# Low ranks, bonus and group mean of RWKV scans as two passes of rounded parts in place of one float32 product

## The chip, the core and the metric

One core of one Trainium2 chip runs the whole program. The time is device microseconds (us) of that core; a kernel's time is the median of its runs. TensorE (PE) multiplies, ScalarE (ACT) and VectorE (DVE) work on tiles in on-chip memory, GpSimd (POOL) does slower elementwise work, and SyncE (SP) issues all loads and stores, in order.

## The reference

A two-layer encoder runs on two sequences (512 and 256 positions, width 1024). Layer 1 has a bidirectional RWKV-7 time mix with 16 heads of 64. What matters here, cut:

```python
g = sigmoid(xg @ g1) @ g2                                   # rank 128
for d in range(2):                                          # forward, backward
    w_log = -softplus(-(w0[d] + tanh(xw @ w1[d]) @ w2[d])) - 0.5      # rank 64
    a = heads(sigmoid(a0[d] + (xa @ a1[d]) @ a2[d]))                  # rank 64
    k_d = k * (1.0 + (a - 1.0) * k_a)
    outs.append(wkv7_scan(r, decay, k_d, v, -kk, kk * a, reverse=(d == 1)))
    bonus.append(sum(r * k_d * r_k, axis=-1, keepdims=True) * v)
y = outs[0] + outs[1]
mean = mean(y, axis=-1); y = (y - mean) * rsqrt(var(y) + eps)         # per head of 64
y = (y * lnx_w + lnx_b + bonus[0] + bonus[1]) * g @ w_o
```

"Second stage" is the product with `w2[d]` or `a2[d]`; the first stage, `xw @ w1`, is made earlier and kept as the low rank tiles.

## The kernel before

Activations lie with features on the 128 partitions and positions along the row. Dense products don't use float32 operands: `split` makes of a tile a rounded part `hi` (type float32r, an ACT copy) and the rest `lo` (a DVE subtraction), and `mms` (L340 to L342) adds three products: hi·hi, hi·lo, lo·hi. The scans' own products are float32, each of which is two matmul instructions in the trace.

`mixer1_scan` works through 12 units: 8 units of two heads for the long sequence (512 positions) and 4 units of four heads for the short one (two tiles of 256 positions). A unit goes through four generators: `prep` (loads k, r, v and the second-stage weights, decay, keys, bonus), `inverse` (the inverse of the chunks' triangular matrices, with many 32x32 products), `scan` (8 chunk steps) and `tail` (group norm, bonus, gate). `weave` interleaves scan of unit u, inverse of u+1, tail of u-1 and prep of u+2 in proportion to given weights. `fill` is dense work with no tie to the scans (feed-forward, projections, memory keys, output projection); `pour` puts pieces of it between the scan's steps. Then a scheduler with its own timing model sets each engine's final order. Every engine works its list in order, so an instruction that waits holds up all behind it.

The places that change, with their names in the trace:

- `second(i, d)` in `prep`, four times a unit: `wide` (L1121) multiplies 64 rows of `w2r` with 64 rows of the rank tile (`l0w`, `l0a`, `l1w`, `l1a`; both directions in one tile, 64 rows each) into a PSUM tile `e`; ACT takes tanh of it (L1158).
- The bonus, once a unit: a DVE product makes `rk` (0/1 block matrix times `r_k`), `wide` multiplies it with `ks` (tile name `th`), and DVE multiplies by v (L1210).
- The mean in `tail`, once a unit: `wide` with the 0/1 matrix `blk` sums y over each head, and DVE subtracts 1/64 of it (L1426).
- The gate's product `g2` with `l0g` or `l1g` also goes through `wide`.
- The low ranks of the long sequence go to memory in `rwkv_in` and are read back at the scans' start; those of the short one are made by `small_low` within `fill`.

Of the kernel before, what the change touches and what calls it, by code (L numbers as in the profile page):

```python
# [37 lines left out]
class Net:  # L38
# [781 lines left out]
    def mixer1_tables(self, c):  # L820
        nc = self.nc
        self.tri = c.tile([128, 2, 128], F32, name="tri2")
        with self.tc.tile_pool(name="tri", bufs=1) as t:
# [3 lines left out]
            for d in range(2):  # L827
                for r in range(2):
                    for q in range(2):
# [12 lines left out]
                             self.par[:, n:n + KT].unsqueeze(1).to_broadcast([128, 12, KT]))  # L842
        self.blk = c.tile([128, 128], F32, name="blk")
        nc.vector.memset(self.blk, 0.0)
        for h in range(2):
            nc.vector.memset(self.blk[64 * h:64 * h + 64, 64 * h:64 * h + 64], 1.0)
        self.id32 = c.tile([128, 32], F32, name="id32")
# [19 lines left out]
    def rwkv_in(self, x, save, L):  # L867
# [97 lines left out]
    def small_low(self, x, L, mix, rstd, nxt):  # L965
# [12 lines left out]
        for j, i in enumerate(LOW):  # L978
            if j == len(LOW) - 1:

                t = self.big("x")
                nc.gpsimd.tensor_copy(t, x[KT - 1])
                x[KT - 1] = t
            ps = [self.pmm.tile([128, self.W], F32, name="mm") for _ in range(2)]
            for r in range(0, KT, 4):
                wr = [[next(ws) for _ in range(4)] for _ in ps]
                for k in range(0, 4, n):
                    for t, w4 in zip(ps, wr):
                        for q in range(k, k + n):
# [4 lines left out]
            t, b = L["wag".index(LOW[i])], self.big("pt")  # L994
# [9 lines left out]
            self.low_end(i, t, t)  # L1004
        yield

# [61 lines left out]
    def head_rsqrt(self, sq, eps, scale, clamp, big, pool):  # L1068
# [3 lines left out]
        for t in range(4):  # L1072
            nc.tensor.matmul(ps[:, t, :], lhsT=sq[:, t * 128:(t + 1) * 128], rhs=self.blk[:, 0:128:64],
                             start=True, stop=True)
# [13 lines left out]

    def mixer1_scan(self, L, rkv, zs, bvs, fill):

# [26 lines left out]
        def wide(lhsT, rhs, pool):  # L1117

            ps = pool.tile([128, W], F32, name="e")
            for (c, l), r in zip(lhsT, rhs):  # L1120
                nc.tensor.matmul(ps[:, c], lhsT=l, rhs=r, start=True, stop=True)  # L1121
            return ps

        def prep(u, o):

            q, parts = units[u]
            np_, p0 = len(parts), parts[0][0]
            Lq = L[q]
            io = {}
# [19 lines left out]
            ks = None  # L1149

            def second(i, d):
                rows = lohi[d]
# [50 lines left out]
            nc.gpsimd.tensor_mul(ks, ks, r)  # L1203
            rks = []
            for p, c in parts:
                rk = ph.tile([128, 128], F32, name="rk", bufs=2)
                nc.vector.tensor_scalar_mul(rk, self.blk, self.p("rw_rk", 0, p))
                rks.append((c, rk))
# [103 lines left out]
        def scan(u, o):  # L1312
# [25 lines left out]
            def ahead(i):  # L1338
# [6 lines left out]
                for d in range(2):  # L1345

                    nc.scalar.activation(uv[:, :, d, :], ps, AF.Copy, scale=self.blk[:, 64 - 64 * d:65 - 64 * d])
                bt = ph.tile([128, 2, 2, 128], F32, name="BT", bufs=2)
# [68 lines left out]
        def tail(u, o):  # L1417

            q, parts = units[u]
            y = o["y"]  # L1420
            bv = tt("bv2")
            nc.sync.dma_start(bv, bvs[u])
            g2 = self.tl.tile([128, 256], F32, name="g2", bufs=1)[:, :128 * len(parts)]
            nc.sync.dma_start(g2, a["rw_g2"][0][:, 128 * parts[0][0]:128 * (parts[-1][0] + 1)])
# [10 lines left out]
            ps = wide([(c, g2[:, 128 * j:128 * j + 128]) for j, (p, c) in enumerate(parts)],  # L1435
                      [L[q][2]] * len(parts), self.pp)
            nc.vector.tensor_mul(y, y, ps)
# [49 lines left out]
    def mixer1(self, l=1):  # L1487
        tc, nc = self.tc, self.nc
        with tc.tile_pool(name="spill", bufs=1, space=bass.MemoryType.DRAM) as dram:
# [4 lines left out]
            bvs = [dt(f"bvs{u}", 512) for u in range(12)]  # L1494
            Ld = [dt(f"l0{n}", SP) for n in "wag"]
            with self.phase():
                self.save_x(xsave, 0)
                g = self.at(SP).rwkv_in([x[:, :SP] for x in self.x], rkv[0], Ld)

# [12 lines left out]
            with tc.tile_pool(name="lora", bufs=1, side="right") as lora, \  # L1512
# [4 lines left out]
                with tc.tile_pool(name="tail", bufs=1, side="right", reuse_waits="tile") as self.tl, self.phase(), ExitStack() as c:  # L1517
                    L = [[lora.tile([128, s1 - s0], F32, name=f"l{q}{n}") for n in "wag"] for q, (s0, s1) in enumerate(SEQS)]
                    for d, t in zip(Ld, L[0]):
                        nc.sync.dma_start(t, d)  # L1520
# [4 lines left out]
                    y = self.mixer1_scan(L, rkv, zs, bvs, self.fill(l, f, xsave, rkv, L, zs))  # L1525

# [158 lines left out]
```

## Time and profile before

| | before |
|---|---|
| median of 3 runs (lowest, highest) | 3052.07 us (3044.27, 3055.18) |
| profiled execution: its own time, span in the trace | 3050.94 us, 3049.0 us |
| busy over the span: PE, DVE, ACT, POOL | 2920.7, 1691.6, 1283.1, 669.1 us |
| the scans, 1250 to 2260 us of the span: PE, DVE, ACT busy | 953.53, 544.36, 568.78 us |
| granted TensorE clock in the scans, as a share of full speed | 0.95 |

Busy time of PE counts the modelled drain of a matmul, which overlaps the next; what a product costs PE is the distance from its start to the next one's start. [...]

### The profile page before, as it was taken

To read this page: it belongs to the slowest core of one execution; us is meant where nothing else is said; L and a number is where in the kernel's file an instruction comes from. 1 tells how busy PE (TensorE), PEld (TensorE's weight loads), DVE (VectorE), ACT (ScalarE), POOL (GpSimd) and SP (SyncE) were. 2 spreads that over 40 slices of the span, in tenths; PEclk is the share of its full clock that TensorE was granted. 3 is DMA by queue.
4 is the path that set the end of the run, shared out by engine and by line. 5 is a ranking of instruction groups with operands and counts; after the bars stand their busy time and mean duration, and the time that the engine had idled before them with its cause. 6 is when DMAs were issued, how large, how long until landed. Compare 5 with 4: busy or idle time off the path is not lost.

```text
span 3049.0 us, 55768 instructions
## 1 busy us (share of the span) xinstructions
PE 2920.7 (96%) x22624; PEld 2467.5 (81%) x22624; DVE 1691.6 (55%) x3008; ACT 1283.1 (42%) x2507; POOL 669.1 (22%) x672
## 2 busy tenths in 40 slices
PE   7999999999999989899989999999989999999997
PEld 6888888888888878777877777777778888888886
DVE  8888647464454596455576545544435564334244
ACT  3333435342232376455656665555444342122122
POOL 4124004020000110232473334444353020000001
PEclk9999999999999999999998999999999999999999
DMA  4224332121265667765435553222352112212111
GB/s 127 58 83 136 114 120 92 51 68 56 97 198 189 209 202 241 256 191 148 147 110 156 152 155 94 76 79 71 112 175 74 59 42 70 69 56 70 63 62 56
DMA packets 362144, 349.23 MB, mean 115 GB/s; under 512 B 42528, under 2 KB 291488, under 8 KB 361888
## 3 DMA queue, kind: packets, MB, share of 16 engines
q1 hardware_dynamic: 361888, 345.68, 36.6%
q8 instruction: 177, 2.90, 0.4%
q14 instruction: 79, 0.65, 0.1%
HBM read 269.06 MB, written 71.83 MB: 112 GB/s over the span
## 4 chain that ended last, share of the span: by engine, by line
PE 79%; DVE 10%; DMA 4%; ACT 3%; issue 3%; POOL 1%; SPq 0%; POOLq 0%; DVEq 0%; ACTq 0%
PE mm L340 21%; PE mm L341 20%; PE mm L342 20%; PE C L1336 3%; PE g L1227 2%; PE y L1336 2%; PE e L1121 2%; PE mm L331 1%; PE sm L331 1%; DVE xs L228 1%; DVE lt L1252 1%; DVE wlo L270 1%; DVE xr L1253 1%; PE py L331 1%; DMA tlo<-low 1%
## 5 line engine op out<-in xcount | busy, mean ns | idle before, releaser
L340 PE MATMUL mm<-xs,whi 128*128 128x512 f32 x2128 | 748.6, 353 | 12.1 <-ACT whi L269 11.0
L341 PE MATMUL mm<-xs,whi 128*128 128x512 f32 x2128 | 751.4, 354 | 4.2 <-DVE xs L228 3.0
L342 PE MATMUL mm<-xs,wlo 128*128 128x512 f32 x2128 | 746.8, 351 | 4.2 <-DVE wlo L270 4.1
L269 ACT CAST whi<-wraw 128x512 fp32r<-128x512 f32 (+1 forms) x492 | 301.9, 616 | 838.8 <-PE mm L341 782.3
L270 DVE TENSOR_TENSOR wlo<-wraw,whi 128x512 fp32r<-128x512 f32 (+1 forms) x492 | 364.4, 743 | 399.9 <-ACT whi L269 371.0
L340 PEld LDWEIGHTS mm<-xs,whi 128*128 128x128 f32 x2128 | 403.0, 190 | 69.6 <-ACT whi L269 11.4
L342 PEld LDWEIGHTS mm<-xs,wlo 128*128 128x128 f32 x2128 | 401.4, 189 | 61.8 <-DVE wlo L270 5.9
L341 PEld LDWEIGHTS mm<-xs,whi 128*128 128x128 f32 x2128 | 402.8, 189 | 58.8 <-DVE xs L228 3.9
L192 POOL TENSOR_TENSOR acc<-acc,sq 128x768 f32<-128x768 f32 (+2 forms) x72 | 114.1, 1585 | 1269.4 <-issue 896.0
L341 PE MATMUL mm<-fb,thi 128*128 128x256 f32 (+1 forms) x720 | 232.7, 323 | 1.1 <-DVE fb L225 1.1
L340 PE MATMUL mm<-hid,whi 128*128 128x512 f32 (+1 forms) x528 | 186.1, 356 | 2.3 <-ACT hid L224 2.3
L341 PE MATMUL mm<-hid,whi 128*128 128x512 f32 (+1 forms) x528 | 187.6, 356 | 0.0
L342 PE MATMUL mm<-hid,wlo 128*128 128x512 f32 (+1 forms) x528 | 186.3, 354 | 0.0
L340 PE MATMUL mm<-fb,thi 128*128 128x256 f32 x528 | 167.9, 318 | 9.3 <-ACT thi L301 9.0
L301 ACT CAST thi<-traw 128x512 fp32r<-128x512 f32 (+1 forms) x202 | 122.6, 609 | 115.8 <-PE mm L341 62.2
L342 PE MATMUL mm<-fb,tlo 128*128 128x256 f32 x528 | 156.4, 299 | 6.3 <-DMA tlo<-low 4.5
L341 PEld LDWEIGHTS mm<-fb,thi 128*128 128x128 f32 x720 | 143.5, 199 | 5.4 <-DVE fb L225 1.3
L340 PE MATMUL mm<-fa,thi 128*128 128x512 f32 (+1 forms) x304 | 125.4, 414 | 0.3 <-ACT fa L224 0.2
L340 PEld LDWEIGHTS mm<-fb,thi 128*128 128x128 f32 x528 | 106.0, 201 | 22.4 <-ACT thi L301 13.2
L342 PEld LDWEIGHTS mm<-fb,tlo 128*128 128x128 f32 x528 | 105.7, 201 | 11.1 <-DMA tlo<-low 5.9
L340 PEld LDWEIGHTS mm<-hid,whi 128*128 128x128 f32 x528 | 99.5, 189 | 17.6 <-ACT hid L224 2.7
L342 PE MATMUL mm<-fa,tlo 128*128 128x512 f32 (+1 forms) x304 | 110.5, 364 | 1.7 <-DMA tlo<-low 1.7
(374 smaller groups left out, 5701.9 us busy)
## 6 DMA issues: line engine op xcount, KB each, us to landing
wraw<-in_ffn_wgu_dram SPq DMA_DIRECT2D x44, 1024.0 KB, 5.2
tlo<-low SPq DMA_DIRECT2D x128, 256.0 KB, 3.2
low<-wlo SPq DMA_DIRECT2D x120, 256.0 KB, 2.8
wraw<-in_ffn_wdown_dram SPq DMA_DIRECT2D x23, 1024.0 KB, 5.2
traw<-in_ffn_wgu_dram SPq DMA_DIRECT2D x56, 256.0 KB, 3.7
wraw<-in_ab_w_in_dram SPq DMA_DIRECT2D x24, 512.0 KB, 3.9
wraw<-in_ca_wkv_dram SPq DMA_DIRECT2D x8, 1024.0 KB, 5.6
kvd<-kv SPq DMA_DIRECT2D x32, 256.0 KB, 2.0
```

The source lines that it names most:

```text
L192: nc.gpsimd.tensor_add(acc, acc, sq)
L228: nc.vector.scalar_tensor_tensor(lo, src, g, hi.bitcast(F32), op0=OP.mult, op1=OP.subtract)
L269: nc.scalar.copy(hi[:, :, :m], raw[:, k0:k1, j:j + m])
L270: nc.vector.tensor_sub(lo[:, :, :m], raw[:, k0:k1, j:j + m], hi[:, :, :m].bitcast(F32))
L301: nc.scalar.copy(hi[:, :n], raw[:, :n])
L331: self.nc.tensor.matmul(ps, lhsT=a[u], rhs=b[v], start=k == 0 and j == 0, stop=k == len(pairs) - 1 and j == 2)
L340: nc.tensor.matmul(ps[:, s0:s1], lhsT=wh, rhs=xh[:, s0:s1], start=start and k == 0, stop=False)
L341: nc.tensor.matmul(ps[:, s0:s1], lhsT=wh, rhs=xl[:, s0:s1], start=False, stop=False)
L342: nc.tensor.matmul(ps[:, s0:s1], lhsT=wl, rhs=xh[:, s0:s1], start=False, stop=stop and k == n - 1)
L1121: nc.tensor.matmul(ps[:, c], lhsT=l, rhs=r, start=True, stop=True)
L1227: nc.tensor.matmul(ps[h][:, j, d, :], lhsT=flat(BK[d][lohi[h], c]), rhs=flat(AR[d][lohi[h], c]), start=True, stop=True)
L1336: last[0] = nc.tensor.matmul(o, lhsT=lhsT, rhs=rhs, start=start, stop=False, skip_group_check=True)
```

## The change

Three groups of float32 products become sums of float32r products with 128 rows.

- Second stages. The low rank of each direction is kept as `hi` and `lo` parts, stacked on 64 + 64 rows of one tile (`lw`, `la`). The weights are loaded twice, into both halves of `w2r`, and split into `w2h` and `w2l`. The product is `w2h` with the stacked tile, plus `w2l` with the stacked tile. `fetch` loads and splits one weight at a time, the next one right behind the product that used the last.
- Bonus. `ks` times `r_k` is split into `kh` and `kl` by ACT and DVE; both are multiplied with the 0/1 matrix `blkr`.
- Mean. y is split into `yh` and `yl`; both are multiplied with `cen`, which is the identity minus 1/64 of the block matrix, so that the product is y minus its mean, which DVE copies out. `tail` has one step more.

Gate, variance and all other products stay. The diff, cut:

```diff
+        self.blk = c.tile([128, 2], F32, name="blk")
+        self.blkr, self.cen = [c.tile([128, 128], F32R, name=n) for n in ("blkr", "cen")]
...
-            nc.sync.dma_start(L["wag".index(LOW[i])], t)
+            if LOW[i] == "g":
+                nc.sync.dma_start(L["g"], t)
+            else:
+                for to, part in zip(L[LOW[i]], self.split(t, tag="xl", bufs=8)):
+                    nc.sync.dma_start(to, part.bitcast(F32))
...
-                nc.tensor.matmul(ps[:, c], lhsT=l, rhs=r, start=True, stop=True)
+                n = len(l)
+                for i in range(n):
+                    nc.tensor.matmul(ps[:, c], lhsT=l[i], rhs=r[i], start=i == 0, stop=i == n - 1)
...
+        def low(q):
+            if q not in ranks:
+                s0, s1 = SEQS[q]
+                ranks[q] = {n: [ph.tile([128, SP], F32R, name=f"l{n}{d}", bufs=1)[:, :s1 - s0] for d in range(2)] for n in "wa"}
+                for n, ts in ranks[q].items():
+                    for d, t in enumerate(ts):
+                        for i, p in enumerate(Ld[q][n]):
+                            nc.sync.dma_start(t[64 * i:64 * i + 64].bitcast(F32), p[64 * d:64 * d + 64])
...
-            w2 = ph.tile([128, 2, 256], F32, name="w2r", bufs=1)
-            for i, n in enumerate(("rw_w2", "rw_a2")):
-                for d in range(2):
-                    nc.sync.dma_start(w2[64 * d:64 * d + 64, i, :128 * np_], a[n][0, d][:, 128 * p0:128 * (p0 + np_)])
...
+            def fetch():
+                if order:
+                    i, d = order.pop(0)
+                    w2 = [ph.tile([128, 256], F32R, name="w2" + s, bufs=1)[:, :128 * np_] for s in "hl"]
+                    raw = ph.tile([128, 256], F32, name="w2r", bufs=1)[:, :128 * np_]
+                    for rows in lohi:
+                        nc.sync.dma_start(raw[rows], a[("rw_w2", "rw_a2")[i]][0, d][:, 128 * p0:128 * (p0 + np_)])
+                    nc.scalar.copy(w2[0], raw)
+                    nc.vector.tensor_sub(w2[1], raw, w2[0].bitcast(F32))
+                    w2s.append(w2)
...
-                ps = wide([(c, w2[rows, i, 128 * j:128 * j + 128]) for j, (p, c) in enumerate(parts)],
-                          [Lq[i][rows]] * np_, self.pp)
+                l, w2 = Lq["wa"[i]][d], w2s.pop(0)
+                ps = wide([(c, [t[:, 128 * j:128 * j + 128] for t in w2]) for j, (p, c) in enumerate(parts)],
+                          [(l, l)] * np_, self.pp)
+                fetch()
...
-                nc.vector.tensor_scalar_mul(rk, self.blk, self.p("rw_rk", 0, p))
+                nc.scalar.activation(hi[:, c], ks[:, c], AF.Copy, scale=self.p("rw_rk", 0, p))
+                nc.vector.scalar_tensor_tensor(lo[:, c], ks[:, c], self.p("rw_rk", 0, p), hi[:, c].bitcast(F32),
+                                               op0=OP.mult, op1=OP.subtract)
-            nc.vector.tensor_mul(bv, wide(rks, [ks[:, c] for _, c in parts], self.pp), v)
+            nc.vector.tensor_mul(bv, wide([(slice(0, W), [self.blkr] * 2)], [(hi, lo)], self.pp), v)
...
-            ps = wide([(slice(0, W), self.blk)], [y], self.pp)
-            nc.vector.scalar_tensor_tensor(y, ps, -1.0 / 64, y, op0=OP.mult, op1=OP.add)
+            nc.scalar.copy(hi, y)
+            nc.vector.tensor_sub(lo, y, hi.bitcast(F32))
+            yield
+            ps = wide([(slice(0, W), [self.cen] * 2)], [(hi, lo)], self.pp)
+            nc.vector.tensor_copy(y, ps)
...
-            weave((part(scan, u), 17), (part(inverse, u + 1), 16), (part(tail, u - 1), 4), (part(prep, u + 2), 12))
+            weave((part(scan, u), 17), (part(inverse, u + 1), 16), (part(tail, u - 1), 5), (part(prep, u + 2), 12))
```

The scheduler's order moves with it. On SP at the scans' start (`iok`, `ior`, `iov` are unit 0's k, r, v; `tlo` and `traw` are weights of the fill), before:

```order
L941 DMA r_9432<-pt 128x512
L1133 DMA iok<-k_9433 128x512
L1133 DMA ior<-r_9425 128x512
L1133 DMA iov<-v_9441 128x512
L1138 DMA w2r<-in_rw_w_dram 64x128 x2
L1138 DMA w2r<-in_rw_a_dram 64x128 x2
L303 DMA tlo<-low_7665 128x512
L294 DMA traw<-in_ffn_wgu_dram 128x4x128
```

and now, where `l0wh` and the like are the parts of the long sequence's ranks in memory:

```order
L952 DMA r_9432<-pt 128x512
L1153 DMA lw_11415<-l0wh 64x512
L1153 DMA lw_11415<-l0wl 64x512
L1153 DMA lw_11416<-l0wh 64x512
L1153 DMA la_11417<-l0ah 64x512
...
L1165 DMA iok<-k_9433 128x512
L1165 DMA ior<-r_9425 128x512
L1165 DMA iov<-v_9441 128x512
L1188 DMA w2r<-in_rw_w_dram 64x128 x2
L303 DMA tlo<-low_7665 128x512
```

Eight loads of ranks stand ahead of `iok`, and the two loads of the `a` weights have moved behind the fill's `tlo`.

On ACT, in the first direction of unit 3's prep (`th<-e,half` is the tanh of a second stage, `R` and `uv` belong to the scan's chain of unit 1), before:

```order
L1379 COPY uv<-C 64x128
L1428 ACTIVATE ysq<-y 128x512
L1235 COPY XL_11384<-G 32x128 x4
L1158 ACTIVATE th<-e,half 128x512
L301 CAST thi<-traw 128x512
L1163 ACTIVATE th<-th 128x512
L431 ACTIVATE th<-g 128x256
L1169 ACTIVATE E<-cu 128x8x64
L1171 ACTIVATE cu<-cu 128x512
```

and now:

```order
L1171 ACTIVATE kksq<-kk 128x512
L1316 COPY Y<-g_13473 128x512
L1420 COPY R<-C 128x128
L301 CAST thi<-traw 128x512
L1189 CAST w2h<-w2r 128x128
L1202 ACTIVATE th<-e,half 128x512
L1207 ACTIVATE th<-th 128x512
L1213 ACTIVATE E<-cu 128x8x64
L1423 COPY uv<-C 64x128
```

A cast of the next weight, which waits for its load and for PE's last use of `w2h`, now stands ahead of the tanh, and a `uv` copy of the scan stands behind both.

On PE at the mean of unit 0, before:

```order
L1352 MATMUL e<-ident,bk_12589 128x128
L1121 MATMUL e<-y,blk 128x512
L1336 MATMUL C<-R,Xinv_11383 128x64 x2
L340 MATMUL mm<-fb,thi 128x256
L341 MATMUL mm<-fb,thi 128x256
```

and now:

```order
L342 MATMUL mm<-fb,tlo 128x256
L1140 MATMUL e<-yh,cen 128x512
L1140 MATMUL e<-yl,cen 128x512
L1388 MATMUL e<-ident,v_13963 128x128 x2
L1380 MATMUL y<-G,uv 64x64 x2
L1380 MATMUL C<-uv,BT 64x64 x4
```

The one product stood between a transpose and a product of the scan's own chain; the two passes stand together, behind products of the fill and ahead of the scan's next transposes.

## Rows read from the trace of the kernel before

**Rows 1.** Busy time by engine in the scans: PE, PEld (weight loads), DVE, ACT, POOL, clock, DMA.

```profile
1250.00:2260.00 1010.00, 953.53 (x11785) 768.73 (x11783) 544.36 (x1187) 568.78 (x1286) 408.28 (x470) 0.95 0.44 131
```

**Rows 2.** The chain that ended last, in the scans, by line.

```profile
by line: PE mm L340 9.9%; PE C L1336 9.2%; PE mm L342 7.8%; PE mm L341 7.7%; PE g L1227 6.9%; PE y L1336 6.2%; PE e L1121 6.0%; issue 3.4%; DVE lt L1252 2.9%; DVE xr L1253 2.7%; DMA tlo<-low 1.9%; DMA traw<-in_ffn_wgu_dram 1.7%; DMA traw<-m
```

**Rows 3.** PE's waits in the scans: us in total, times, longest.

```profile
PE C L1336 <- DVE S L1391: 5.9, 9, 1.3
PE C L1336 <- DVE uv L1380: 5.6, 6, 2.4
```

**Rows 4.** Timeline of PE at float32 products of `wide`: start, us, line, operands.

```profile
1253.65 1.12 PE L1121 MATMUL e<-l0w,w2r 64*128 64x512 f32 x2
1254.70 0.38 PE L340 MATMUL mm<-fb,thi 128*128 128x256 f32 x1
...
1292.86 1.02 PE L1121 MATMUL e<-th,rk 128*128 128x512 f32 x2
1293.81 1.16 PE L1227 MATMUL g<-ar,bk 64*128 64x128 f32 x8
...
1428.88 1.02 PE L1121 MATMUL e<-y,blk 128*128 128x512 f32 x2
1429.74 0.56 PE L1336 MATMUL C<-R,Xinv 128*128 128x64 f32 x4
...
1829.67 1.13 PE L1121 MATMUL e<-l1w,w2r 64*128 64x256 f32 x4
1830.72 0.34 PE L1336 MATMUL y<-G,uv 128*64 128x64 f32 x4
```

**Rows 5.** Timeline of PE at the fill's float32r products (types print as f32).

```profile
2240.55 0.47 PE L340 MATMUL mm<-fa,thi 128*128 128x512 f32 x1
2240.87 0.40 PE L341 MATMUL mm<-fb,thi 128*128 128x512 f32 x1
2241.10 0.39 PE L342 MATMUL mm<-fa,tlo 128*128 128x512 f32 x1
...
2246.37 0.28 PE L340 MATMUL mm<-fb,thi 128*128 128x256 f32 x1
2246.49 0.28 PE L341 MATMUL mm<-fb,thi 128*128 128x256 f32 x1
```

**Rows 6.** A group of weight loads: count, then busy us, mean ns, idle.

```profile
L340 PEld LDWEIGHTS mm<-fa,thi 128*128 128x128 f32 x304 | 59.5, 196 | 13.0 <-issue 7.4 <-ACT fa L224 0.7 <-DVE xr L1253 0.2
```

**Rows 7.** Groups of ACT and DVE like those added, in the scans.

```profile
L1376 ACT COPY R<-C 128x128 f32<-128x128 f32 x96 | 25.3, 263 | 48.8 <-PE C L1336 47.8
L224 ACT CAST fb<-xi 128x256 fp32r<-128x256 f32 x24 | 9.6, 403 | 2.2 <-DVE xi L899 1.1 <-PE mm L342 0.9
L224 ACT CAST fa<-zt 128x512 fp32r<-128x512 f32 x8 | 4.9, 618 | 5.0 <-DMA zt<-zs 4.9
...
L225 DVE TENSOR_TENSOR fb<-xi,fb 128x256 fp32r<-128x256 f32 x24 | 12.3, 521 | 6.7 <-ACT fb L224 6.5
L225 DVE TENSOR_TENSOR fb<-zt,fa 128x512 fp32r<-128x512 f32 x8 | 6.0, 754 | 7.9 <-ACT fa L224 7.9
...
L1207 DVE TENSOR_SCALAR rk<-blk,par 128x128 f32<-128x128 f32 x16 | 5.2, 328 | 10.0 <-PE e L1121 10.0
```

**Rows 8.** SP: issue ns (min/median/max) and landing of `w2r`; its longest wait in the scans.

```profile
L1138 SPq DMA_DIRECT2D w2r<-in_rw_w_dram x24: 472/552/1346, 1248.9 to 2027.0; - x24
...
DMA to landing us min/median/max: 2.2/3.1/4.1
...
SPq L303 <- PE mm L342: 182.5, 88, 10.2
```

**Rows 9.** Timeline of PE just behind the scans' start.

```profile
1257.93 0.39 PE L342 MATMUL mm<-fb,tlo 128*128 128x256 f32 x1 [0.96 <-DMA tlo<-low]
```

**Rows 10.** One stretch at the low clock (columns as in rows 1), and PE just ahead of it.

```profile
1722.50:1732.70 10.20, 9.95 (x94) 7.69 (x93) 1.47 (x3) 5.94 (x12) 2.36 (x2) 0.50 0.39 111
...
1718.95 1.56 PE L1277 MATMUL g<-XL,Y 32*32 32x32 f32 x121 [0.32 <-issue]
```

More of the change, by code (lines that the diff above doesn't have):

```diff
@@ L842, in mixer1_tables @@
                              self.par[:, n:n + KT].unsqueeze(1).to_broadcast([128, 12, KT]))
[L843 to L846, printed above, removed]
+        self.blk = c.tile([128, 2], F32, name="blk")
+        self.blkr, self.cen = [c.tile([128, 128], F32R, name=n) for n in ("blkr", "cen")]
+        with self.tc.tile_pool(name="blks", bufs=1) as t:
+            blk = t.tile([128, 128], F32, name="blkt")
+            nc.vector.memset(blk, 0.0)
+            for h in range(2):
+                nc.vector.memset(blk[64 * h:64 * h + 64, 64 * h:64 * h + 64], 1.0)
+            nc.vector.tensor_copy(self.blk, blk[:, 0:128:64])
+            nc.scalar.copy(self.blkr, blk)
+            nc.vector.scalar_tensor_tensor(self.cen, blk, -1.0 / 64, self.ident, op0=OP.mult, op1=OP.add)
         self.id32 = c.tile([128, 32], F32, name="id32")
@@ L993, in small_low @@
                     yield
-            t, b = L["wag".index(LOW[i])], self.big("pt")
+            t, b = L["g"] if LOW[i] == "g" else self.big("pt"), self.big("pt")
             nc.scalar.copy(t, ps[0])
@@ L1004, in small_low @@
             self.low_end(i, t, t)
+            if LOW[i] != "g":
+                hi, lo = [p.bitcast(F32R) for p in (self.nrm.tile([128, self.W], F32, name="acc", bufs=1), self.big("pt"))]
+                nc.scalar.copy(hi, t)
+                nc.vector.tensor_sub(lo, t, hi.bitcast(F32))
+                for to, part in zip(L[LOW[i]], (hi, lo)):
+                    nc.sync.dma_start(to, part.bitcast(F32))
         yield
@@ L1072, in head_rsqrt @@
         for t in range(4):
-            nc.tensor.matmul(ps[:, t, :], lhsT=sq[:, t * 128:(t + 1) * 128], rhs=self.blk[:, 0:128:64],
+            nc.tensor.matmul(ps[:, t, :], lhsT=sq[:, t * 128:(t + 1) * 128], rhs=self.blk,
                              start=True, stop=True)
@@ L1087, in head_rsqrt, with mixer1_scan @@
         return out
-    def mixer1_scan(self, L, rkv, zs, bvs, fill):
+    def mixer1_scan(self, L, Ld, rkv, zs, bvs, fill):
         nc, a, ph = self.nc, self.a, self.ph
@@ L1120, in wide @@
             for (c, l), r in zip(lhsT, rhs):
-                nc.tensor.matmul(ps[:, c], lhsT=l, rhs=r, start=True, stop=True)
-            return ps
+                n = len(l)
+                for i in range(n):
+                    nc.tensor.matmul(ps[:, c], lhsT=l[i], rhs=r[i], start=i == 0, stop=i == n - 1)
+            return ps
+        ranks = {}
+        def low(q):
[6 more added lines that the diff above has]
+                            nc.sync.dma_start(t[64 * i:64 * i + 64].bitcast(F32), p[64 * d:64 * d + 64])
+            return ranks[q]
         def prep(u, o):
@@ L1127, in prep @@
             np_, p0 = len(parts), parts[0][0]
-            Lq = L[q]
+            Lq = low(q)
             io = {}
@@ L1149, in prep @@
             ks = None
+            w2s, order = [], [(i, d) for d in range(2) for i in range(2)]
+            def fetch():
[9 more added lines that the diff above has]
+            fetch()
             def second(i, d):
-                rows = lohi[d]
                 th = t6("th")
-                ps = wide([(c, w2[rows, i, 128 * j:128 * j + 128]) for j, (p, c) in enumerate(parts)],
-                          [Lq[i][rows]] * np_, self.pp)
+                l, w2 = Lq["wa"[i]][d], w2s.pop(0)
+                ps = wide([(c, [t[:, 128 * j:128 * j + 128] for t in w2]) for j, (p, c) in enumerate(parts)],
+                          [(l, l)] * np_, self.pp)
+                fetch()
                 for p, c in parts:
@@ L1203, in prep @@
             nc.gpsimd.tensor_mul(ks, ks, r)
[L1204 removed]
+            hi, lo = t6("kh").bitcast(F32R), t6("kl").bitcast(F32R)
             for p, c in parts:
[L1206 to L1208 removed]
+                nc.scalar.activation(hi[:, c], ks[:, c], AF.Copy, scale=self.p("rw_rk", 0, p))
+                nc.vector.scalar_tensor_tensor(lo[:, c], ks[:, c], self.p("rw_rk", 0, p), hi[:, c].bitcast(F32),
+                                               op0=OP.mult, op1=OP.subtract)
             bv = t6("bv")
[L1210 removed]
+            nc.vector.tensor_mul(bv, wide([(slice(0, W), [self.blkr] * 2)], [(hi, lo)], self.pp), v)
             nc.sync.dma_start(bvs[u], bv)
@@ L1345, in ahead @@
                 for d in range(2):
-                    nc.scalar.activation(uv[:, :, d, :], ps, AF.Copy, scale=self.blk[:, 64 - 64 * d:65 - 64 * d])
+                    nc.scalar.activation(uv[:, :, d, :], ps, AF.Copy, scale=self.blk[:, 1 - d:2 - d])
                 bt = ph.tile([128, 2, 2, 128], F32, name="BT", bufs=2)
@@ L1420, in tail @@
             y = o["y"]
+            g2 = self.tl.tile([128, 256], F32, name="g2", bufs=1)[:, :128 * len(parts)]
+            nc.sync.dma_start(g2, a["rw_g2"][0][:, 128 * parts[0][0]:128 * (parts[-1][0] + 1)])
+            hi, lo = tt("yh").bitcast(F32R), tt("yl").bitcast(F32R)
+            nc.scalar.copy(hi, y)
[3 more added lines that the diff above has]
+            nc.vector.tensor_copy(y, ps)
             bv = tt("bv2")
             nc.sync.dma_start(bv, bvs[u])
-            g2 = self.tl.tile([128, 256], F32, name="g2", bufs=1)[:, :128 * len(parts)]
-            nc.sync.dma_start(g2, a["rw_g2"][0][:, 128 * parts[0][0]:128 * (parts[-1][0] + 1)])
-            ps = wide([(slice(0, W), self.blk)], [y], self.pp)
-            nc.vector.scalar_tensor_tensor(y, ps, -1.0 / 64, y, op0=OP.mult, op1=OP.add)
             sq = tt("ysq")
@@ L1434, in tail @@
             yield
-            ps = wide([(c, g2[:, 128 * j:128 * j + 128]) for j, (p, c) in enumerate(parts)],
-                      [L[q][2]] * len(parts), self.pp)
+            ps = wide([(c, [g2[:, 128 * j:128 * j + 128]]) for j, (p, c) in enumerate(parts)],
+                      [[L[q]["g"]]] * len(parts), self.pp)
             nc.vector.tensor_mul(y, y, ps)
@@ L1494, in mixer1 @@
             bvs = [dt(f"bvs{u}", 512) for u in range(12)]
-            Ld = [dt(f"l0{n}", SP) for n in "wag"]
+            Ld = [{n: [dt(f"l{q}{n}{s}", s1 - s0) for s in "hl"] for n in "wa"} for q, (s0, s1) in enumerate(SEQS)]
+            Ld[0]["g"] = dt("l0g", SP)
             with self.phase():
                 self.save_x(xsave, 0)
-                g = self.at(SP).rwkv_in([x[:, :SP] for x in self.x], rkv[0], Ld)
+                g = self.at(SP).rwkv_in([x[:, :SP] for x in self.x], rkv[0], Ld[0])
                 for _ in range(2):
@@ L1517, in mixer1 @@
                 with tc.tile_pool(name="tail", bufs=1, side="right", reuse_waits="tile") as self.tl, self.phase(), ExitStack() as c:
-                    L = [[lora.tile([128, s1 - s0], F32, name=f"l{q}{n}") for n in "wag"] for q, (s0, s1) in enumerate(SEQS)]
-                    for d, t in zip(Ld, L[0]):
-                        nc.sync.dma_start(t, d)
+                    L = [dict(g=lora.tile([128, s1 - s0], F32, name=f"l{q}g")) for q, (s0, s1) in enumerate(SEQS)]
+                    nc.sync.dma_start(L[0]["g"], Ld[0]["g"])
+                    L[1].update(Ld[1])
                     pool = lambda name, bufs: c.enter_context(tc.tile_pool(name=name, bufs=bufs, space=PSUM, reuse_waits="tile"))
@@ L1524, in mixer1 @@
                         setattr(self, n, pool(n, 1))
-                    y = self.mixer1_scan(L, rkv, zs, bvs, self.fill(l, f, xsave, rkv, L, zs))
+                    y = self.mixer1_scan(L, Ld, rkv, zs, bvs, self.fill(l, f, xsave, rkv, L, zs))
                     z = [f.split(t) for t in y]
```

## The prediction

> **What bounds the kernel now.** The change lies almost wholly in the scans, so I read them first as one stretch: busy time by engine [rows 1]. PE is busy 953.5 of 1010 us, 94%; DVE and ACT are at 54 and 56%. So PE is the bound there, with 56.5 us of idle time, and the other two have room if their work comes at the right moment. The chain of work that ended last shows where PE's time decides [rows 2]: `wide`, line L1121, has 6.0% of the stretch, 60.6 us. What stops PE is spread thin; the waits for DVE are typical, 5.9 and 5.6 us in all over a few occurrences [rows 3]. Nothing but PE work can give much here.
>
> **What is removed.** A product's price on PE is the distance to the next start. A float32 second stage of 512 columns and 64 rows starts at 1253.65 and the next product at 1254.70: 1.05 us. For the short sequence, two tiles of 256 columns in one stage, it is 1830.72 - 1829.67 = 1.05 us as well. The bonus takes 1293.81 - 1292.86 = 0.95 us, the mean 1429.74 - 1428.88 = 0.86 us [rows 4]. A unit has four second stages, one bonus and one mean, and there are 12 units: 48 x 1.05 + 12 x 0.95 + 12 x 0.86 = 72.1 us.
>
> **What stands in its place.** The fill shows what a float32r pass of 128 rows costs in a steady stream: 0.23 us for 512 columns, 0.12 us for 256. A first pass behind a float32 product takes 2240.87 - 2240.55 = 0.32 us, 0.09 more [rows 5]. Two passes over 512 columns are 0.46 to 0.47 us, and four over 256 the same. So the changed products need 72 x 0.466 = 33.6 us if all run at the steady price and 6.5 us more if each pays an entry. PE loses between 72.1 - 40.1 = 32.0 and 72.1 - 33.6 = 38.5 us of work. Most of the old products stand between other float32 work, so entries will be paid now and then, but the float32 price in those rows holds such a change of kind too; I take 38.5.
>
> **How much of that is time.** L1121's products, with the 12 gate products that stay, taken at the bonus's 0.95 us, fill 72.1 + 11.4 = 83.5 us, and 60.6 of them lie on the chain: 0.73. Off the chain, a shorter product only lengthens the idle time behind it. So 0.73 x 38.5 = 28 us, with 0.73 x 32.0 = 23 as the lower and 38.5 as the upper bound. I take 28.
>
> **What is added on ACT and DVE.** ACT gets 32 casts of 128x128 (0.263 us each), 16 of 128x256 (0.403) and, for the bonus and the mean, 24 times 512 columns (0.618): 8.4 + 6.4 + 14.8 = 30 us. DVE gets 32 subtractions at about 0.328, 16 at 0.521 and 24 at 0.754, less the 16 `rk` products of 0.328 that go: 10.5 + 8.3 + 18.1 - 5.2 = 32 us [rows 7]. The copy behind the mean costs what the subtraction there cost. Both engines go up by about 6% of what they do in the scans, and stay at 60% or less. If PE's idle time of 56.5 us grows in that proportion, it is 3 us. The lower bound is nothing. The upper bound is that each of the 72 products waits for its own cast and subtraction: 24 x 1.37 + 32 x 0.59 + 16 x 0.92 = 67 us, which I hold far from the truth, since a weight is fetched right behind the product that used the last one, and PE has the fill to work on meanwhile. Queued behind such a cast on ACT are the scan's `R` and `uv` copies, and PE waits for them; this is the rival below.
>
> **What is added on SP.** The weights are loaded twice, 48 loads more; the ranks take 8 writes and 16 reads in place of 2 and 2, 20 more. These 68 at about 0.55 us are 37 us of issuing over the scans and the stage ahead. SP stands waiting for a free `tlo` buffer alone for 182.5 us [rows 8], so I cost them at nothing, except at the scans' start. There eight rank loads stand ahead of unit 0's inputs and ahead of `tlo`, and two weight loads have moved behind it: 6 x 0.55 = 3 us later, at a place where PE waited 0.96 us for exactly such a `tlo` [rows 9]. I charge 3 us; the bounds are 0, if the fill still has products to run, and 6, if the late `traw` behind it is waited for as well. Without that slack on SP, the 68 issues would cost up to 37 us.
>
> **At nothing.** The splits of the ranks ahead of the scans and inside the fill (a cast and a subtraction each, under 1.4 us) stand beside dense products. The last mean, with 1.37 us more of casts and subtractions ahead of it, has the fill's products beside it, such as those from 2246.37 on [rows 5]; without them it would cost its 1.4 us. The tail's fifth step and the later load of the bonus only move work that is not on the chain.
>
> **The sum.** -28 + 3 + 3 = -22 us against the profiled execution's own time of 3050.94 us (span 3049.0), which is 1.1 us under the median of the runs: **3029 us**, 0.8% less than 3052.07. About 0.5%, 15 us, is what a measurement of this kernel can tell from no change.
>
> **Rivals.**
>
> *All of it lands.* PE is 94% busy, the scheduler orders the work anew with the shorter products, and nothing else grows: -38.5 us, 3012 us; with a little less time at the low clock down to 3003. Against it stands that a quarter of these products lay off the chain.
>
> *The cover is gone.* Each long product covered a wait behind it, so idle time takes half of the lower gain: -16 + 6 = -10, 3041 us, with 3037 to 3052 for this whole case. For it: PE's waits are many and short [rows 3].
>
> *Loads in front of the scan's copies (slower).* Each `w2r` load has one buffer: it is issued only when the split before it is done, takes 0.55 us to issue and 3.1 us to land [rows 8], and the ACT cast stands in ACT's list ahead of `uv` copies. If the load is late, ACT stands still, then the scan's chain, then PE. There are 48 such fetches. At 22 / 48 = 0.46 us of PE idle time for each, the gain is gone; from 37 / 48 = 0.8 us on the kernel is slower by over 0.5%; at 1 us it takes 3077 us. Against it: 48 fetches share 1010 us, 21 us for each on average, several times the load.
>
> [...]
>
> *Weight loads in series.* Each of the passes has a weight load of its own, 0.196 us [rows 6]. If it did not overlap, a pair over 512 columns would cost 2 x (0.233 + 0.196) = 0.86 us and a short-sequence stage 4 x (0.12 + 0.196) = 1.26 us: 32 x 0.19 - 16 x 0.21 + 12 x 0.09 = 4 us gained, less 6 added, about 3052 us. The fill's passes start every 0.23 and 0.12 us [rows 5], the latter less than a load, so the loads overlap there. [...]
>
> **How the numbers follow.** The forecast, 3018 to 3037 us, has a chance of 0.44; all of it lands, 3003 to 3018, 0.20; cover gone 0.22; late loads 0.07; the clock 0.05, three fifths of it slower; loads in series 0.02. Faster by over 0.5% (under 3037) is 0.44 + 0.20 = 0.64; within 0.5% is 0.22 + 0.02 + 0.02 = 0.26; slower is 0.07 + 0.03 = 0.10. The range of 8 in 10 goes from 3003, where all lands, to 3048, most of the case without cover; outside lie the slower cases and the ends of the others.
>
> **What would show it.** Right: the second stages, bonus and mean each take 0.46 to 0.56 us from start to next start; PE busy in the scans falls by 30 to 39 us, the scans end 20 to 30 us earlier, and their idle time is 56 to 70 us; ACT and DVE are busy some 30 us more each. Wrong: passes of 0.4 us apiece (loads in series); ACT waits for `w2r` loads of tens of microseconds in sum and PE waits behind `uv` (late loads); a mean clock under 0.93 (the clock); idle time of PE over 75 us (cover gone). The prediction as a whole would fall if the stages before 1250 or after 2260 moved by more than a few microseconds, since it gives them nothing.

## The result and the profile after

The changed kernel takes 3100.12 us (median of 4 runs, 3098.02 to 3103.36), the kernel before 3049.24 us (4 runs): a ratio of 1.0167, 95% interval 1.0144 to 1.0190. It is slower by 51 us; the forecast was 3029 us. The profiled execution took 3103.36 us, its span is 3101.6.

The scans after, by engine (columns as in [rows 1]), from unit 0's first step to the last unit's y; and one stretch at the low clock:

```profile
1267.90:2293.10 1025.20, 927.62 (x11639) 768.85 (x11638) 574.00 (x1228) 582.31 (x1344) 397.95 (x461) 0.92 0.42 126
...
1635.60:1662.90 27.30, 27.30 (x141) 23.06 (x139) 10.34 (x17) 11.16 (x30) 14.78 (x15) 0.50 0.27 76
```

The same stretch of before:

```profile
1249.90:2240.80 990.90, 937.70 (x11679) 754.82 (x11678) 537.63 (x1174) 561.16 (x1271) 397.42 (x460) 0.95 0.43 128
```

Read them as a sum. Length less busy time is PE's idle time: 53 us before, 98 after. The stretches that the trace records at a granted clock of 0.50, called the low clock here, add up to 96 us before and 160 after; here are their sums, before and after (length, then PE's busy time):

```profile
sum 95.57, PE 91.73 PEld 77.53 DVE 43.33 ACT 45.63 POOL 35.05; mean PE 7.06 PEld 5.96 DVE 3.33 ACT 3.51 POOL 2.70
```

```profile
sum 160.43, PE 139.36 PEld 118.13 DVE 80.97 ACT 77.88 POOL 60.63; mean PE 9.95 PEld 8.44 DVE 5.78 ACT 5.56 POOL 4.33
```

How much of PE's busy time in them is lost can be read from products that also ran at 1.00. After the change, at 0.50:

```profile
1659.29 0.41 PE L340 MATMUL mm<-fb,thi 128*128 128x256 f32 x1
1659.50 0.41 PE L341 MATMUL mm<-fb,thi 128*128 128x256 f32 x1
...
1660.85 0.78 PE L1140 MATMUL e<-lw,w2h 128*128 128x512 f32 x1
1661.42 0.63 PE L1140 MATMUL e<-lw,w2l 128*128 128x512 f32 x1
1661.98 0.48 PE L1380 MATMUL y<-G,uv 128*64 128x64 f32 x4
```

A fill pass of 256 columns takes 0.21 us from start to start in place of 0.12, a pair of passes between scan products 1.13 in place of 0.66 (at 1487.98, below). Before, a bonus in the stretch of [rows 10] took 1732.85 - 1730.85 = 2.00 us in place of 0.95. So 0.42 to 0.53 of the time is lost; half is taken from here on, an estimate.

What is left is PE's work at full clock: 937.7 - 91.7 / 2 = 892 us before, 927.6 - 139.4 / 2 = 858 after. So work fell by 34 us, idle time grew by 44, the low clock took 24 more by that estimate, and the scans became 34 us longer. The other 18 us lie ahead of them: unit 0's first step came at 1267.9, not 1249.9. Behind the scans nothing moved (808 us from the last y to the end, both times).

The changed products, as in [rows 4] (start, us, line, operands):

```profile
1285.42 0.40 PE L1140 MATMUL e<-la,w2h 128*128 128x512 f32 x1
1285.65 0.40 PE L1140 MATMUL e<-la,w2l 128*128 128x512 f32 x1
...
1487.98 0.50 PE L1140 MATMUL e<-lw,w2h 128*128 128x512 f32 x1
1488.32 0.40 PE L1140 MATMUL e<-lw,w2l 128*128 128x512 f32 x1
1488.64 0.45 PE L1380 MATMUL C<-uv,BT 128*64 128x64 f32 x8
...
2130.82 0.28 PE L1140 MATMUL e<-lw,w2h 128*128 128x256 f32 x1
2130.94 0.28 PE L1140 MATMUL e<-lw,w2l 128*128 128x256 f32 x1
2131.06 0.28 PE L1140 MATMUL e<-lw,w2h 128*128 128x256 f32 x1
2131.18 0.28 PE L1140 MATMUL e<-lw,w2l 128*128 128x256 f32 x1
2131.30 0.55 PE L1380 MATMUL C<-R,Xinv 128*128 128x64 f32 x4
```

Behind products of the fill, a pass starts 0.23 us behind the one ahead at 512 columns, and four take 0.48 us at 256. The weight loads overlap: one takes 0.19 us (median of `w2h`'s and `w2l`'s), more than the 0.12 from start to start. Between float32 products of the scan, as at 1487.98, a pair takes 0.66 us: 0.34 for its first pass, 0.32 to the scan's next product. Summed over the trace from start to next start, less idle time and with half of what ran at the low clock, the changed products took 71 us before and 43 after: 28 us less. The scans have 40 matmuls fewer, of which 8 are these products' own. The other 32 are products of the fill that ran ahead of unit 0's first step; they make up most of the 6 us between 28 and 34.

In the chain that ended last, `wide` (now L1140, gate included) fell from 6.0 to 2.7%:

```profile
by line: PE mm L340 9.5%; PE C L1380 8.7%; PE g L1271 8.1%; PE mm L342 7.7%; PE mm L341 7.7%; PE y L1380 5.3%; issue 4.8%; DMA traw<-in_ffn_wgu_dram 2.9%; PE e L1140 2.7%; DVE xr L1297 2.6%; DVE lt L1296 2.1%; PE e L1090 1.8%; PE g L1349 1.
```

PE's longest waits, 1250 to 2300 us, as in [rows 3]:

```profile
PE C L1380 <- DVE S L1435: 14.4, 16, 2.4
PE C L1380 <- DVE uv L1424: 11.6, 11, 3.9
PE mm L342 <- DMA tlo<-low: 10.2, 9, 3.0
PE g L1340 <- DVE X L1323: 8.1, 1, 8.1
PE g L1315 <- DVE X L1305: 7.5, 4, 4.5
```

In the scans alone, the rows of this view sum to 53 us for DVE (23 before), 23 for ACT (16), 10 for DMA (7). For the casts and subtractions that the change adds, PE waited at its products 3.8 us in all:

```profile
PE e L1140 <- ACT w2h L1189: 1.8, 1, 1.8
PE e L1140 <- DVE yl L1469: 1.3, 3, 0.6
PE e L1140 <- ACT kh L1250: 0.4, 1, 0.4
PE e L1140 <- DVE kl L1251: 0.3, 1, 0.3
```

So most of the new idle time lies at the scan's and the inverse's own steps: `S` and `uv` have 26 us in place of 11.5, `X` has 16 in place of 4. The longest single wait shows how far a cause can lie from its place: PE and DVE (idle time ahead in brackets), then the chain ahead of them:

```profile
1594.59 1.92 PE L1340 MATMUL g<-X,G 32*32 32x32 f32 x64 [8.12 <-DVE X L1323]
...
1592.71 0.69 DVE L298 TENSOR_TENSOR traw<-traw,gmu 128x512 f32<-128x512 f32 x1 [2.74 <-DMA traw<-in_rw_w_dram]
1593.32 0.48 DVE L1322 SCALAR_TENSOR_TENSOR XL<-g,lanes,XL 128x256 f32<-128x256 f32 x1
1593.83 0.71 DVE L1323 STREAM_TRANSPOSE X<-XL 128x512 f32<-128x512 f32 x1
...
1582.23 0.89 POOL tlo L305
1583.12 3.20 DMA traw<-in_rw_g_dram
1586.34 0.70 DVE traw L298
1587.12 0.63 ACT thi L301
...
1587.82 1.27 POOL tlo L305
...
1589.53 2.71 DMA traw<-in_rw_w_dram
```

The fill's own weights stand here one behind the other: a `traw` load waits for POOL's subtraction of the weight ahead of it, DVE waits for the load in front of the inverse's steps, and PE stands behind DVE. SP had also stood five microseconds at a `w2r` load, up to 1582.54, but the `traw` load behind it was released only at 1583.12, by POOL; the new loads are not on this chain.

### The profile page after: what moved, and what is told of

Its sections match the earlier page's. It is cut to its first block, busy times and chain, and to the rows that moved or that the text cites. A ratio compares the mean times of both kernels' runs of the same rounds, so it can differ in the third digit from the quotient of the medians.

```text
span 3101.6 us, 56093 instructions
## 1 busy us (share of the span) xinstructions
PE 2921.1 (94%) x22616; PEld 2490.1 (80%) x22616; DVE 1737.7 (56%) x3074; ACT 1308.5 (42%) x2588; POOL 671.3 (22%) x672
## 4 chain that ended last, share of the span: by engine, by line
PE 76%; DVE 11%; DMA 5%; ACT 3%; issue 3%; POOL 1%; SPq 1%; DVEq 0%; POOLq 0%; ACTq 0%
PE mm L340 20%; PE mm L341 20%; PE mm L342 19%; PE C L1380 3%; PE g L1271 3%; PE y L1380 2%; DMA traw<-in_ffn_wgu_dram 1%; PE mm L331 1%; PE sm L331 1%; DVE xs L228 1%; DVE wlo L270 1%; PE e L1140 1%; DVE xr L1297 1%; PE py L331 1%; DVE lt L1296 1%
```

## The experiments

**Theory.** At first: the single-buffered weight (load, cast, subtraction) holds up SP and DVE, PE waits, and the clock falls with the idle time (98 us idle and 160 us at the low clock, in place of 53 and 96). **Rivals:** short products alone do it (idle time and low clock eat what they save); the added work on ACT or DVE does it; any other order of the scheduler does it.

All runs, each against the kernel before on its own chip. The last four columns are us of the profiled execution, from unit 0's first step to the last y (work as worked out above; time at the low clock and PE's busy time in it summed from the trace; a profiled execution can lie off its median, e10's by 17 us, e5's, e8's and e14's by 10 or 11):

| run | median | ratio, 95% | scans | idle | low clock | work |
|---|---|---|---|---|---|---|
| before | 3049 | | 991 | 53 | 96 | 892 |
| changed | 3100 | 1.0144 to 1.0190 | 1025 | 98 | 160 | 858 |
| e1 stages only | 3095 | 1.0059 to 1.0173 | 1033 | 76 | 188 | 867 |
| e2 sums only | 3088 | 1.0061 to 1.0136 | 1025 | 69 | 147 | 885 |
| e3 two buffers | 3111 | 1.0140 to 1.0218 | 1041 | 94 | 191 | 859 |
| e4 ready weights | 3091 | 1.0097 to 1.0150 | 1002 | 85 | 133 | 857 |
| e5 short alone | 3066 | 1.0013 to 1.0061 | 1019 | 69 | 156 | 875 |
| e6 long, added work | 3107 | 1.0134 to 1.0198 | 1030 | 82 | 133 | 885 |
| e7 passes twice | 3106 | 1.0131 to 1.0194 | 1028 | 84 | 113 | 892 |
| e8 order | 3060 | 0.9999 to 1.0032 | 1007 | 54 | 130 | 892 |
| e9 no subtractions | 3079 | 1.0046 to 1.0100 | 1004 | 86 | 136 | 857 |
| e10 on POOL | 3098 | 1.0076 to 1.0160 | 1006 | 85 | 126 | 863 |
| e11 ranks later | 3102 | 1.0113 to 1.0170 | 1036 | 93 | 187 | 856 |
| e12 casts twice | 3110 | 1.0135 to 1.0196 | 1035 | 93 | 181 | 857 |
| e13 mean only | 3068 | 1.0027 to 1.0084 | 1006 | 62 | 126 | 883 |
| e14 bonus only | 3061 | 1.0008 to 1.0054 | 989 | 59 | 99 | 884 |
| e15 stages ready | 3094 | 1.0091 to 1.0181 | 1014 | 73 | 149 | 872 |
| e16 keys on POOL | 3052 | 0.9983 to 1.0027 | 989 | 53 | 102 | 890 |
| e17 subtractions twice | 3104 | 1.0149 to 1.0196 | 1034 | 97 | 164 | 860 |
| e18 order, second | 3024 | 0.9895 to 0.9935 | 964 | 38 | 61 | 897 |

**Parts alone.** e1 has the changed kernel's `fetch` and ranks with the old bonus and mean (one `rk` buffer in place of two); e2 the reverse; e13 and e14 are e2's halves.

> Only the second stages are changed; the bonus and the mean are float32 products again. Loads theory (the weight's load, cast and subtraction have one buffer each, so SP stands at the next load and the fill's loads stand behind it): nearly the whole loss is here, 3085 to 3100 us. Shortness theory (a shorter product leaves PE idle behind it, and idle time brings the low clock): 48 of the 72 products are here, so two thirds of the loss, about 3083 us. Casts theory (the added casts and subtractions on ACT and DVE, 16 of about 30 us each on an engine are the second stages'): about half, 3075 us.

> Only the bonus and the mean are changed; the second stages are float32 products of 64 rows again. Loads theory: no w2r load is split here, so no loss, 3035 to 3052 us. Shortness theory: 24 of 72 products, a third of the loss, about 3066 us. Casts theory: half of the loss, about 3075 us.

> The kernel before with only the group norm's mean changed (12 casts, 12 subtractions, 12 copies in place of 12 subtractions, and the tail's fifth step). Added DVE time is 12.7 us. If each microsecond that DVE gets more is lost one for one: 3063 to 3070 us. If the mean is the costly half of the two sums (its cast, subtraction, passes and copy follow one another behind the end of the scan's unit): 20 us or more over the kernel before.

> The kernel before with only the bonus changed. DVE gets 9 us of subtractions more and 5 us of r_k products less, so 4 us. If DVE's time is what counts: within 5 us of the kernel before. If the added cast and subtraction in the middle of prep delay the bonus and what stands behind it: 15 us or more over it.

Both halves lose, 1.2 and 1.0%, and don't add up (1.7%). That fits no theory alone: the loads theory gave e2 nothing to lose. The mean alone loses 0.6%, the bonus alone 0.3%.

**Loads.** e3, e4, e11 and e15 (e4's weights and e11's move, with the old bonus and mean):

```diff
# e3
+ w2.append([ph.tile([128, 128], F32R, name="w2" + s, bufs=2) for s in "hl"])
+ raw = ph.tile([128, 128], F32, name="w2r", bufs=2)
...
# e4: split once in rwkv_in, both parts side by side in memory
+ t = ph.tile([128, 2, 128], F32R, name="w2", bufs=3)
+ nc.sync.dma_start(t.bitcast(F32), self.w2d[i, d][:, p0 + j])
# e11
- Lq = low(q)
  io = {}
...
  k, r, v = io["k"], io["r"], io["v"]
+ Lq = low(q)
```

> As the changed kernel, but the raw weight and its two parts have two buffers of 128 columns each, and for the eight long-sequence units the weights are fetched two ahead; the four short units keep one weight ahead, in two pieces. Loads theory: SP's wait at the w2r load falls from about 85 us to under 40, PE idle time in the scans from 100 to about 75 us, and half or more of the loss in units 0 to 7 comes back: 3060 to 3080 us. Shortness and casts theories: the products and the casts are the same, so 3090 to 3105 us.

> As the changed kernel, but the weights are split once in the stage ahead of the scans and kept in memory; a fetch in the scans is then one load of both parts, with no cast, no subtraction and three buffers. Loads theory: the loss in the scans' units is gone, 3035 to 3065 us, of which 10 to 13 us are the ranks' loads at the scans' start. Shortness theory: the products are as short as in the changed kernel, so still 3085 us or more. Casts theory: the second stages' half of the added work is gone, about 3075 us.

> The changed kernel with the eight loads of the ranks asked for behind unit 0's k, r and v in place of ahead of them. Start theory (13 us of the loss lie ahead of unit 0's first step, most of it behind these loads): unit 0's first step 4 to 8 us earlier, 3090 to 3096 us. If the first second stage waits for its ranks just as long, no change: 3098 to 3103 us.

> Only the second stages changed, with both parts of ranks and weights made ahead of the scans, one load for a weight, and the ranks asked for behind unit 0's inputs: the scans have the short products and no cast or subtraction more. Clock theory (shorter products turn into idle time and low clock whatever stands beside them): 3055 to 3075 us, with 140 us or more at the low clock in the scans. If the added work is all of the loss: 3025 to 3045 us.

With two buffers nothing came back, so the single buffer is not what costs: the loads theory fell. Nor did ACT, whose cast comes first, stand still for these loads in the changed kernel: it waited 3.8 us for them in the whole of the scans.

```profile
ACT w2h L1189 <- DMA w2r<-in_rw_w_dram: 2.2, 4, 0.9
ACT w2h L1189 <- DMA w2r<-in_rw_a_dram: 1.6, 3, 0.9
```

SP's longest wait of this kind did shrink, in the changed kernel and in e3:

```profile
SPq L1188 <- DVE w2l L1190: 44.8, 18, 11.9
```

```profile
SPq L1190 <- DVE w2l L1192: 34.0, 18, 3.7
```

e4's scans are 23 us shorter than the changed kernel's, but their first step is 8 us later (12 without what the two profiles differ by ahead of 1080 us, where both programs are the same): making the weights ahead costs time there. e15 starts late too (1271 us), and with no cast or subtraction in the scans beyond before it still has 149 us at the low clock. e11 starts unit 0 at 1259.3, 8.6 us earlier, of which 4.4 arose ahead of 1080 us as well; its ratio is lower, but the intervals overlap.

**Length against added work.** e5 has the short products of the second stages without the work, e6 and e7 the work without the short products. e5 leaves out the rests of both operands, and its second pass adds the first one again; e6 leaves the rests out of the products:

```diff
# e5, on the kernel before; operands rounded ahead of the scans
+ w2 = ph.tile([128, 2, 256], F32R, name="w2r", bufs=1)
...
+ n = 2 if l.dtype == F32R else 1
+ for i in range(n):
+     nc.tensor.matmul(ps[:, c], lhsT=l, rhs=r, start=i == 0, stop=i == n - 1)
# e6
+ nc.tensor.matmul(ps[:, c], lhsT=f(l[0]), rhs=f(r[0]), start=True, stop=True)   # f: as float32
# e7
+ for _ in range(n):
      for i in range(n):
...
```

> The kernel before, with the second stages alone as two float32r passes of 64 rows over the same rounded operands (the rests of both operands are left out, and the second pass repeats the first); the weights are rounded once in the stage ahead and loaded as before, so that the scans have no cast, no subtraction and no load more than before. Shortness theory (PE's saved time becomes idle time and low clock): at least as slow as with only the second stages changed, 3070 to 3100 us, with PE idle time in the scans near 75 us and over 140 us at the low clock. Added-work theory (casts, subtractions and loads delay the scans): all of the saving and none of the loss, 3015 to 3040 us.

> The changed kernel with all its loads, casts and subtractions, but each changed product is one float32 product of the first parts (the rests are left out of the products, though still made), as long on PE as before. Shortness theory: back to about the time of before, 3045 to 3065 us. Added-work theory: slower still than the changed kernel, by PE's 30 us, about 3110 to 3130 us.

> The changed kernel with each pair of passes made twice into the same sums, so that a changed product takes about 0.93 us of PE, near the 0.86 to 1.05 us of before; nothing else is added. Shortness theory: 3045 to 3070 us. Added-work theory: 3110 to 3130 us.

Both sides were half right. e5's work is 17 us less, and none of it arrives: 69 us idle and 156 us at the low clock. e7 has 34 us more work than the changed kernel and takes about the same time: 14 us less idle, 48 us less at the low clock. e6, with 27 us more, takes about the same as well. So PE's 34 us do not decide, in either direction. But the added work with long products costs 50 us as well:

```profile
1250.10:2269.00 1018.90, 950.23 (x11679) 779.20 (x11679) 539.85 (x1174) 558.94 (x1271) 399.03 (x460) 0.92 0.42 124
```

```profile
1263.40:2290.90 1027.50, 943.70 (x11805) 783.77 (x11806) 580.04 (x1227) 584.39 (x1343) 399.70 (x460) 0.95 0.43 126
```

The first row is e5, the second e7. e5 has before's DVE and ACT time and the clock of the changed kernel; e7 has the work of before, the mean clock of before and the idle time of the added work.

**DVE or ACT.** e9, e10, e12, e17 change the scans' added elementwise work (e9 leaves the rests out), e16 is the kernel before with one product for the keys moved to POOL:

```diff
# e9: the second pass uses the first part again
- nc.vector.tensor_sub(w2[1], raw, w2[0].bitcast(F32))     # and kl, yl
...
# e10
+ nc.gpsimd.tensor_sub(w2[1], raw, w2[0].bitcast(F32))     # and yl
...
# e12: twice
+ nc.scalar.copy(w2[0], raw)                               # and kh, yh
...
# e17: twice
+ nc.vector.tensor_sub(w2[1], raw, w2[0].bitcast(F32))     # and kl, yl
...
# e16
+ nc.gpsimd.tensor_mul(bk[:, :, 1 - d, :], c8(th), c8(Ei))
```

> The changed kernel without its 72 pairs' subtractions on DVE in the scans: the second pass repeats the first part (the rests are left out); loads, casts, passes and their number stay. DVE theory (PE's waits for DVE rose from 23 to 56 us in sum, and those for ACT not at all, so the subtractions delay DVE's own steps of the scan): PE's waits for DVE back to 23 to 35 us and 25 to 35 us of the time back, 3065 to 3075 us. ACT or load theory: 3090 to 3105 us, since the casts and the loads are all still there.

> The changed kernel with the subtractions for the weights and for y on POOL, those of the bonus still on DVE: 23 of the 29 us that the subtractions take of DVE are gone from it. DVE theory: 20 to 28 us back, if the passes don't wait for POOL instead, 3072 to 3085 us; if POOL's longer subtraction is waited for, nothing. ACT or load theory: 3095 to 3110 us.

> The changed kernel with each of the scans' added casts on ACT made twice, 30 us more of ACT's time and nothing else. DVE theory: PE does not wait for ACT more than before the change (23 us), so 0 to 8 us, 3100 to 3108 us. ACT theory (the added casts are what costs): 20 to 35 us more, 3120 to 3135 us.

> The changed kernel with each of the scans' added subtractions on DVE made twice: 37 us more of DVE's time and nothing else. DVE theory (without them 29 us came back): 20 to 40 us more than the changed kernel, a ratio to before of 1.023 to 1.030. If it is not DVE's time but only the wait of a pass for its own second part, the dose counts just as much for the passes but not for the scan's steps: 0 to 10 us more, 1.017 to 1.020.

> The kernel before with one of DVE's products in prep, 24 of 0.82 us for the keys, made on POOL: 19.7 us of DVE's time fewer in the scans, some 31 us of POOL's more. DVE theory turned round: PE waits less for DVE and the kernel is 8 to 25 us faster than before. If the later keys are waited for instead (POOL takes longer, and the first products of the inverse need them): 0 to 15 us slower.

e9 looked like proof: 29 us back (0.94% of 3061). But its idle time is 86 us, hardly less than 98, PE's waits for DVE still sum to 42 us, and the dose says no. e17 gives DVE 616.6 us of work in the scans in place of 574.0, and its ratio is 1.0173 against 1.0167:

```profile
1263.50:2297.00 1033.50, 936.86 (x11631) 775.25 (x11632) 616.60 (x1302) 582.05 (x1344) 398.35 (x459) 0.92 0.42 125
```

Twice the casts cost nothing either (e12, 21 us more of ACT's time), 21 us less on DVE gave nothing that can be told (e10, its interval overlaps the changed kernel's), and 14 us of DVE's time taken from the kernel before gave nothing (e16). Each of these kernels also got an order of its own, which can hide some of a cost (see below); but none of the four shows one. So time on ACT or DVE does not look like the bound: the DVE theory fell, as a matter of DVE's time. What a subtraction that stands and waits costs stays possible: DVE stood 27.2 us at `w2l` for its cast in the changed kernel.

```profile
DVE w2l L1190 <- ACT w2h L1189: 27.2, 13, 5.5
```

**Order alone.** The kernel before, with one weight of `weave` changed: the tail's 4 to 5 (e8; the change itself does this too), the scan's 17 to 18 (e18).

> The kernel before, with the tail's weight in the weave 5 in place of 4 and nothing else: the same instructions in another order. If the loss is that of the changed work, 3045 to 3060 us. If any other order than the one of before costs this much (order theory), 3065 us or more.

> The kernel before, with the scan's weight in the weave 18 in place of 17 and nothing else. Order theory, as in the first control: 3050 to 3062 us if an order costs little by itself; 3070 us or more if the order of before is a lucky one, and then the differences of under 20 us between the experiments carry no weight.

e8 moved nothing that can be told; e18 made the kernel 0.85% faster, 3024 us, with the same instructions. It is the fastest version seen, and beats both kernels:

```profile
1251.40:2214.90 963.50, 925.50 (x11679) 743.19 (x11678) 535.77 (x1174) 560.17 (x1270) 400.23 (x460) 0.97 0.43 131
```

38 us idle and 61 us at the low clock: an order alone is worth 15 us of idle time and 34 us of low clock. So a single difference of up to some 30 us between two of these kernels, e9's included, says nothing of its cause. The sign of the loss is another matter. The ten kernels with all three places changed, some in part (the changed one, e3, e4, e6, e7, e9 to e12, e17), lie from 1.007 to 1.018, the four without (before, e8, e16, e18) from 0.992 to 1.002.

## Why the prediction was wrong

- **What stands in its place** was mis-sized: 72 products at the steady 0.466 us are 33.6 us, 40.1 with an entry each; they took 43. The saving of 38.5 us measured 28, under the lower bound of 32.0. A steady price holds between products of the fill; next to the scan's own products both ends of a pair cost more (0.34 and 0.32 us at 1487.98, 0.23 in the fill). "Weight loads in series" was rightly held unlikely.
- **"How much of that is time"** is the step that failed for the sign. A share of 0.73 of the chain was taken to be time; e5, e6 and e7 show about none of PE's saving arriving. A row of the chain says what ended last in one order. It does not say that the next limit lies 28 us away.
- **"If PE's idle time of 56.5 us grows in that proportion, it is 3 us"** failed worst: it grew by 44. The busy shares of ACT and DVE, 60% or less, were right and beside the point, and the copy behind the mean did cost what the subtraction there had (0.69 us each). Doubling their added work costs nothing that can be told, yet idle time rises with the number of places changed: 53 to 54 us in before, e8 and e16 (38 in e18), 59 to 76 with a part of the change (e1, e2, e5, e13 to e15), 82 to 98 with all of it. That each product would wait for its own cast and subtraction was rightly held far from the truth (3.8 us); the idle time came at the scan's and the inverse's own steps, which the sum did not charge.
- **The clock** was priced apart from idle time, at 0.05, three fifths of it slower. No run shows that split; what the runs show is 61 (e18) to 191 us (e3) at the low clock in the scans. Low clock and idle time came together: 44 us more idle and 65 us more at the low clock, counted as 24 us. "The cover is gone" and "the clock" were one case, and their sum, 68 us, takes the 34 us that PE's work fell by and 34 us more.
- **The scans' start** was given 3 us; it is 13. Of the 18, 5 arose ahead of 1080 us, where both programs are the same; the rest behind the ranks' splits (5 by 1150 us) and ahead of the first step, where the eight loads stand. The statement that nothing ahead of the scans would move fell with it.
- **SP at nothing** holds as far as e3 goes. "Loads in front of the scan's copies" had the right sign by another way: its single buffer is not the cause, and ACT waited 3.8 us for the loads in place of tens.

Open: what makes the idle time. It is not only hand-overs between engines: e5 and e15 add no cast and no subtraction to the scans and are 69 and 73 us idle. One row sum divides the runs: PE's waits for DVE are 22 to 33 us in the eight kernels with the old mean (before, e1, e5, e8, e14 to e16, e18) and 34 to 60 in the twelve with the new one. Ten of these twelve have everything else changed too, so this points to the mean without proving it. e9 points to the subtractions and e4 to the weights' casts and loads, but order alone moves as much. Holding the order fixed while one piece goes was not tried, nor the changed kernel with e18's weight.

## What to carry to other kernels

Before a saving on the busiest engine is counted as time, ask what the idle time becomes, and charge idle time with the low clock that the traces show beside it: here 65 us more of it came with 44, counted as 24. Read a share of the chain as an upper bound for a gain, not as an estimate: here 0.73 of the saving was counted, and none came. Price a product where it will stand, not in a steady stream. Where a scheduler writes the order, time one or two neutral changes of it first: here they moved the kernel by 0.2 and 0.85%, and the parts of the change by 0.3 to 1.2%.

## What was not expected of the hardware

The low clock can last through work without a gap: PE was busy 27.30 of 27.30 us in the stretch from 1635.6 shown above, at 0.50 throughout. Just ahead of it, PE had waited 1.40 us for DVE and started products on 64 rows:

```profile
1634.74 1.34 PE L1271 MATMUL g<-ar,bk 64*128 64x128 f32 x8 [1.40 <-DVE G L1274]
```

What sets the clock is not shown. At the two ends of idle time the low clock goes with it: 160 us in the changed kernel, with 98 us idle, and 61 in e18, with 38. Idle time is not all of it: e7, with 84 us idle but long products, has 113 us, and e5, with 69 us idle and short ones, 156. That short products draw it is not shown, though, since e8 has 130 us at 54 us of idle time with the products of before.

The same program can get a different clock: e1 took 3101 us at a mean granted clock of 0.961 and 3063 us at 0.975.
